# Sliding-window attention kept feature-major, three norms summed late, and every row scale from four narrow products: a two-layer decoder trunk on one core

## The chip, the cores and the metric

The kernel runs on one core of a Trainium2 chip. A core has a matrix engine (PE in the profile, its weight loads PEld), a vector engine (DVE), a scalar engine (ACT), a general engine (POOL) and an engine whose queue here only issues transfers (SP). The engines run side by side and wait for one another through semaphores; each works its own list of instructions in order. The metric is the device time of one launch in microseconds (us); a smaller number is better.

## The reference

Two macaron layers over 512 tokens of 1024 features, all in float32, and one norm at the end:

```
for i in 0, 1:
    h = h + 0.5 * swiglu(rms_norm(h, ln_ffn1[i]), ffn1_w_in[i], ffn1_w_out[i])      # 1024 -> 2 x 2816 -> 1024
    u = rms_norm(h, ln_mix[i])
    h = h + (mamba2(u) if i == 0 else sliding_window_attention(u))
    h = h + 0.5 * swiglu(rms_norm(h, ln_ffn2[i]), ffn2_w_in[i], ffn2_w_out[i])
out = rms_norm(h, final_norm)

rms_norm(x, w) = x * rsqrt(mean(x * x) + 1e-6) * w
swiglu(x, w_in, w_out) = (silu(gate) * up) @ w_out,  gate, up = split(x @ w_in)
attention: q, k, v = u @ w_qkv + b_qkv (16 query heads of 64, 4 key/value heads), rotary on q and k;
    logits = q k^T / 8 within the last 128 tokens; probs = softmax over the logits and one sink per head;
    out = (probs @ v) @ w_o + b_o
```

So there are seven row scales `rsqrt(mean(h*h) + eps)`: one ahead of each of the four feed-forward blocks, one ahead of each mixer and a last one.

## The kernel before

**Layout.** `h` lies feature-major: eight tiles `h0..h7` of 128 features by 512 tokens. The products are done to near float32 accuracy by splitting both sides into a rounded half and a rest (`hi`, `lo`) and doing three products of 512 columns (`mm3`, L328 to L330). `project` (L332) makes one 128 by 512 output from the eight `x` tiles: 24 products. The row scale is not applied to `x`; it multiplies the outputs when they leave PSUM, so a projection may run before its scale is known.

**Weights** stream from memory in the order of `weight_plan` into two raw buffers; ACT makes `whi` (L215), DVE `wlo` (L216), with four buffers each; the loads stand in SP's queue, beside `h` at the start.

**A norm's sum.** `make_x` (L258) is called when a tile `h[k]` is final: ACT scales it to `x` hi (L264), DVE makes `x` lo (L265), ACT squares it (L276) and POOL adds the square to `ss` (L277). The row scale from `ss` comes in two ways. `row_scale` (L312) splits `ss`, sums over the partitions with two products of 512 columns against a matrix of ones (L319, L320; the result stands in all partitions), and DVE takes the inverse root by three Newton steps on 128x512 tiles. `token_scale` (L291) does four products with one column (`psn`), so that the result is 128x4, DVE takes the root on that, and `spread` (L302) brings it to 128x512 with four products against the identity (`psb`) and a copy by ACT. Before, the first feed-forward block and the Mamba mixer take the second way, the other three blocks and the attention the first.

**Attention** (`swa`). Tokens of `SWA_ORDER` are walked: `K`, `V`, `Q` project, `v` turns V to token-major, `O` is a part of the output projection, and `a`, `b`, `c`, `d` are the steps of the generator `attend` for a pair of heads t. In `a`, PE makes the logits of both heads (`pss`, one head behind the other, L757), DVE adds the mask and finds the maximum (L761), ACT does the exponentials with their sum (L768). In `b`, PE turns the 2 x 7 blocks of probabilities (`pp`, L777) and ACT copies them out (`pT`). In `c`, PE multiplies the turned probabilities with the values, tokens on the partitions (`pav`, L787 and L789), and DVE multiplies with one over the sum (L792). In `d`, PE turns that back to feature-major (`pot`, L796), ACT and DVE split it to hi and lo. PSUM tiles come from two pools: `mm` with 4 buffers and `big` with 2; `pss`, `pp` and the tiles of the row scales are `big`.

**Order.** The program's text gives each engine its instructions; the framework then lists them anew per engine at compile time, by its own model of readiness. An engine never goes past an instruction that waits.

Of the kernel before, what the change touches and what calls it, by code (L numbers as in the profile page):

```python
# [18 lines left out]
S = 512  # L19
# [37 lines left out]


MAMBA_ORDER = mamba_order()
SWA_ORDER = """K0 V0 Q0 Q1 v0 a0 Q2 b0 a1 Q3 b1 c0 a2 K1 b2 c1 d0 a3 V1 b3 c2 d1 Q4 c3 d2 v1 O0:0 O0:1 Q5 d3 a4 Q6 b4 a5  # L60
O0:2 O0:3 Q7 b5 c4 a6 O1:0 O1:1 b6 c5 d4 a7 O1:2 O1:3 b7 c6 d5 O2:0 O2:1 c7 d6 O2:2 O2:3 d7 O3:0 O3:1 O3:2 O3:3
""".split()


def parse(tok):
    n, _, q = tok[1:].partition(":")
    return tok[0], int(n), int(q or 0)


def rows(k):  # L70
# [78 lines left out]
def trunk(ctx: ExitStack, tc: tile.TileContext, xT, pos, wflat, params, consts, out):  # L149
# [105 lines left out]
    x = [None] * KT  # L255
    norm = {}

    def make_x(k, n):  # L258
        w = pcol(P_LN + n * 8 + k)
        if k == 0:  # L260
            norm["ss"] = sm([128, S], name="ss", bufs=1)
# [9 lines left out]
        ss = norm["ss"]  # L271
        if k == 0:
            act.activation(ss, h[k], AF.Square)  # L273
        else:
            sq = t2([128, S], name="sq")
            act.activation(sq, h[k], AF.Square)  # L276
            pool.tensor_add(ss, ss, sq)  # L277

    def rsqrt(y, v, n, alloc):
        sh = alloc([128, n], I32, name=f"sh{n}")  # L280
# [28 lines left out]
        act.copy(rbc, pb)  # L309
        return rbc  # L310

    def row_scale():  # L312
        ss = norm["ss"]
        hi = t2([128, S], F32R, name="sshi")
        lo = t2([128, S], F32R, name="sslo")
        act.copy(hi, ss)
        dve.tensor_sub(lo, ss, hi.bitcast(F32))
        ps = big([128, S], name="psv")
        pe.matmul(ps, ones, hi, start=True, stop=False)  # L319
        pe.matmul(ps, ones, lo, start=False, stop=True)  # L320
        v = t2([128, S], name="nvw")
        dve.tensor_scalar(v, ps, EPS, None, op0=ALU.add)
        rbc = sm([128, S], name="rbc", bufs=1)
        rsqrt(rbc, v, S, t2)
        return rbc
# [6 lines left out]
    def project(eng=None):  # L332
# [4 lines left out]
            mm3(ps, hi[:, sl], lo[:, sl], (x[k][:, 0, :], x[k][:, 1, :]), k == 0, k == KT - 1)  # L337
        return ps

    def ffn(nxt, aside=None):  # L340
        gs = []
        for i in range(FT):
            if i == 8 and aside:
                aside()
            if i == 0 and nxt == 1:
                pg, pu = mm([128, S]), mm([128, S])
                for k in range(KT):
                    if k % 2 == 0:
                        hi, lo = next_w()
                    for j, ps in enumerate((pg, pu)):  # L350
                        sl = slice((2 * (k % 2) + j) * 128, (2 * (k % 2) + j + 1) * 128)
                        mm3(ps, hi[:, sl], lo[:, sl], (x[k][:, 0, :], x[k][:, 1, :]), k == 0, k == KT - 1)
                rbc = spread(token_scale(big, [norm["ss"]], 0, 4))
            else:
                pg = project()
                if i == 0:
                    rbc = row_scale()
                pu = project()
            t = t2([128, S], name="t")
            dve.tensor_mul(t, pg, rbc)  # L360
            act.activation(t, t, AF.Silu)
            dve.tensor_mul(t, pu, t)  # L362
            if i % 2 == 0:
                gs += halves("g")
            act.copy(gs[i][0], t)
            dve.tensor_sub(gs[i][1], t, gs[i][0].bitcast(F32))
# [347 lines left out]
        return cs, sn  # L714

    def swa(nxt, cs, sn):
        rbc = None
# [4 lines left out]
        def evac(b):  # L722
            nonlocal rbc
            ps = project()
            if rbc is None:
                rbc = row_scale()
            t = m4([128, S], name="qkv")
# [12 lines left out]
        def attend(t):  # L740
# [5 lines left out]
            rinv = sm([128, 4, 2], name="rinv")  # L746
            lgs = []
            for a in range(2):
                hs = slice(64 * a, 64 * a + 64)
                sink = pcol(P_SK + 2 * t + a)  # L750
                pss = big([128, 4, 256], name="pss")
                lg = m4([128, 4, 256], name="lg")
                lgs.append(lg)
                for i in range(4):
                    k0 = max(i - 1, 0) * 128
                    o = 128 if i == 0 else 0
                    pe.matmul(pss[:, i, o:], q[hs, i * 128:(i + 1) * 128], kT[kv][hs, k0:(i + 1) * 128],  # L757
                              start=True, stop=True)
                for i in range(4):
                    o = 128 if i == 0 else 0  # L760
                    dve.tensor_tensor_reduce(lg[:, i, o:], pss[:, i, o:], mask[:, o:], scale=0.125,  # L761
                                             scalar=-3.0e38, op0=ALU.add, op1=ALU.max,
                                             accum_out=mx[:, a, i:i + 1])
# [7 lines left out]
                dve.reciprocal(rinv[:, :, a], den[:, a, :])  # L771
            yield
            pTs = []
            for a in range(2):
# [7 lines left out]
            po = mm([128, 4, 2, 64], name="pav")  # L782
            for a in range(2):
                hs = slice(64 * a, 64 * a + 64)
                for i in range(4):
                    if i:
                        pe.matmul(po[:, i, a, :], pTs[a][:, 2 * i, :], vtok[kv][:, i - 1, hs],  # L787
                                  start=True, stop=False)
                    pe.matmul(po[:, i, a, :], pTs[a][:, 2 * i + 1, :], vtok[kv][:, i, hs],  # L789
                              start=i == 0, stop=True)  # L790
# [9 lines left out]
            act.copy(yt[0], pt)  # L800
            dve.tensor_sub(yt[1], pt, yt[0].bitcast(F32))
            yield

        chains = {}
        for tok in SWA_ORDER:
            s, n, part = parse(tok)
            if s == "Q":
                qT[n] = rope(evac(n))
            elif s == "K":
                kT[n] = rope(evac(8 + n))  # L810
            elif s == "V":
                vT = evac(10 + n)
            elif s == "v":
                pv = mm([128, 4, 128], name="pv")
                for c in range(4):
# [3 lines left out]
            elif s == "a":  # L819
                chains[n] = attend(n)  # L820
                next(chains[n])
            elif s in "bcd":
                next(chains[n])
            else:
                out_proj(part, n, pairs[n], n == 3, nxt, P_BO)
# [80 lines left out]
```

## Time and profile before

| | us |
|---|---|
| median of the runs (3; 2113.33 to 2117.11) | 2115.55 |
| the profiled execution, whole | 2119.48 |
| its span | 2117.7 |
| PE busy | 2083.3 (98%) |
| DVE busy | 1111.9 (53%) |
| ACT busy | 736.7 (35%) |
| POOL busy | 198.4 (9%) |

The profile's page comes first: busy times, the span in 40 slices, and the chain that ended last, of which PE is 91% and DVE 7%. With PE busy nearly throughout, what is left to look for is of three kinds: products that could go, stretches in which PE waits, and stretches in which its granted clock is at the lower level. Matmuls are pipelined: a row's own duration is longer than its distance to the next start, so distances between starts are used for the price of a product.

### The profile page before, as it was taken

Reading aid. Unit: us, or ns where it says so; the run is one execution under the profiler, and the core shown is the slowest. Engines: PE = TensorE matmul, PEld = TensorE weight load, DVE = VectorE, ACT = ScalarE, POOL = GpSimd, SP = SyncE. Lnnn points to the kernel's source line nnn. Section 1 sums busy time; section 2 is a strip of 40 time slices with the busy share of each in tenths; the row PEclk is TensorE's granted clock in tenths of the full one; section 3 lists DMA queues with packets and bytes.
Section 4 is the critical chain, followed back from the end, with each engine's and each line's share of the span. In section 5 each row is a group of like instructions: output and inputs, shape, how many; then the busy total and the mean of one; then the engine's idle time right before and its main releaser. Section 6 shows DMA issues by size and latency. Waiting matters only on the chain.

```text
span 2117.7 us, 24898 instructions
## 1 busy us (share of the span) xinstructions
PE 2083.3 (98%) x9967; PEld 1736.5 (82%) x9967; DVE 1111.9 (53%) x1709; ACT 736.7 (35%) x1088; POOL 198.4 (9%) x142
## 2 busy tenths in 40 slices
PE   8999999999999999999999999999999999999998
PEld 6888888888888887888888888888878878888887
DVE  6433433677888888443433535443365675334333
ACT  4332222454444444332222323322236443222222
POOL 2000001223222222000000000000110120000000
PEclk9999999999999999999999999999999999999999
DMA  5333232323333322333323333333321213333231
GB/s 163 95 100 100 88 100 84 115 90 107 100 97 98 92 83 80 93 97 99 97 92 93 97 100 100 94 97 92 96 93 41 60 51 99 100 100 92 92 98 67
DMA packets 58867, 197.62 MB, mean 93 GB/s; under 512 B 6656, under 2 KB 6912, under 8 KB 58752
## 3 DMA queue, kind: packets, MB, share of 16 engines
q1 hardware_dynamic: 58608, 196.03, 30.1%
q8 instruction: 78, 1.28, 0.2%
q14 instruction: 37, 0.30, 0.0%
q10 hardware_dynamic: 144, 0.00, 0.0%
HBM read 193.85 MB, written 2.16 MB: 93 GB/s over the span
## 4 chain that ended last, share of the span: by engine, by line
PE 91%; DVE 7%; ACT 1%; issue 1%; DMA 1%; POOL 0%; SPq 0%; ACTq 0%; DVEq 0%; POOLq 0%
PE mm L328 27%; PE mm L330 27%; PE mm L329 27%; PE psz L648 1%; PE psz L650 1%; PE psz L649 1%; PE psy L590 1%; DVE wlo L216 1%; DVE x L265 1%; PE pss L757 1%; DVE acc L518 1%; PE pav L789 1%; PE pp L777 1%; PE pav L787 0%; PE pso L593 0%
## 5 line engine op out<-in xcount | busy, mean ns | idle before, releaser
L215 ACT CAST whi<-wraw 128x1024 fp32r<-128x1024 f32 (+2 forms) x355 | 364.7, 1029 | 1084.2 <-PE mm L329 725.7
L328 PE MATMUL mm<-x,whi 128*128 128x512 f32 x1760 | 692.6, 394 | 5.8 <-DVE whi L213 5.7
L329 PE MATMUL mm<-x,whi 128*128 128x512 f32 x1760 | 690.0, 392 | 5.9 <-DVE x L265 5.9
L330 PE MATMUL mm<-x,wlo 128*128 128x512 f32 x1760 | 689.2, 392 | 1.1 <-DVE wlo L216 1.0
L216 DVE TENSOR_TENSOR wlo<-wraw,whi 128x1024 fp32r<-128x1024 f32 (+3 forms) x329 | 395.0, 1201 | 299.9 <-ACT whi L215 288.0
L329 PEld LDWEIGHTS mm<-x,whi 128*128 128x128 f32 x1760 | 332.7, 189 | 77.5 <-DVE x L265 9.1
L328 PEld LDWEIGHTS mm<-x,whi 128*128 128x128 f32 x1760 | 332.8, 189 | 76.3 <-ACT ss L273 5.7
L330 PEld LDWEIGHTS mm<-x,wlo 128*128 128x128 f32 x1760 | 332.6, 189 | 72.4 <-DVE wlo L216 2.0
L328 PE MATMUL mm<-ga,whi 128*128 128x512 f32 (+1 forms) x726 | 283.2, 390 | 0.0
L330 PE MATMUL mm<-ga,wlo 128*128 128x512 f32 (+1 forms) x726 | 280.7, 387 | 0.0
L329 PE MATMUL mm<-gb,whi 128*128 128x512 f32 (+1 forms) x726 | 279.4, 385 | 0.0
L277 POOL TENSOR_TENSOR ss<-ss,sq 128x512 f32<-128x512 f32 x48 | 72.5, 1510 | 1489.2 <-ACT sq L276 1487.9
L362 DVE TENSOR_TENSOR t<-mm,t 128x512 f32<-128x512 f32 x88 | 60.9, 692 | 270.2 <-PE mm L330 269.7
L360 DVE TENSOR_TENSOR t<-mm,rbc 128x512 f32<-128x512 f32 x88 | 60.6, 691 | 214.1 <-PE mm L330 213.1
L330 PEld LDWEIGHTS mm<-ga,wlo 128*128 128x128 f32 x726 | 136.2, 188 | 32.1
L329 PEld LDWEIGHTS mm<-gb,whi 128*128 128x128 f32 x726 | 136.2, 188 | 30.3
L328 PEld LDWEIGHTS mm<-ga,whi 128*128 128x128 f32 x726 | 136.1, 187 | 29.3
L216 POOL TENSOR_TENSOR wlo<-wraw,whi 128x1024 fp32r<-128x1024 f32 x30 | 73.4, 2448 | 218.1 <-ACT whi L215 218.1
L518 DVE SCALAR_TENSOR_TENSOR acc<-xp,par,acc 128x512 f32<-128x512 f32 x96 | 85.4, 889 | 1.4 <-ACT acc L516 1.3
L648 PE MATMUL psz<-whi,x 128*128 128x256 f32 x224 | 64.9, 290 | 5.3 <-DVE xp L514 5.3
L445 DVE TENSOR_TENSOR h<-mm,h 128x512 f32<-128x512 f32 x88 | 59.5, 685 | 14.0 <-PE mm L330 13.8
L650 PE MATMUL psz<-whi,x 128*128 128x256 f32 x224 | 64.1, 286 | 0.0
(211 smaller groups left out, 1902.1 us busy)
## 6 DMA issues: line engine op xcount, KB each, us to landing
wraw<-wflat SPq DMA_DIRECT2D x320, 512.0 KB, 3.6
wraw<-wflat SPq DMA_DIRECT2D x32, 384.0 KB, 3.0
abc<-actr SPq DMA_DIRECT2D x32, 256.0 KB, 5.0
h<-xT SPq DMA_DIRECT2D x8, 256.0 KB, 3.8
out<-out SPq DMA_DIRECT2D x4, 512.0 KB, 2.7
wraw<-wflat SPq DMA_DIRECT2D x4, 256.0 KB, 3.1
wraw<-wflat SPq DMA_DIRECT2D x2, 432.0 KB, 3.2
cst<-consts SPq DMA_DIRECT2D x1, 321.5 KB, 3.8
```

Of the source, the lines that this page charges most:

```text
L215: act.copy(hi[:, :w], r[:, :w])
L216: (eng or dve).tensor_sub(lo[:, :w], r[:, :w], hi[:, :w].bitcast(F32))
L277: pool.tensor_add(ss, ss, sq)
L328: pe.matmul(ps, whi, xt[0], start=first, stop=False)
L329: pe.matmul(ps, whi, xt[1], start=False, stop=False)
L330: pe.matmul(ps, wlo, xt[0], start=False, stop=last)
L360: dve.tensor_mul(t, pg, rbc)
L362: dve.tensor_mul(t, pu, t)
L445: dve.tensor_add(h[m], ps, h[m])
L518: dve.scalar_tensor_tensor(acc, xp[:, j:j + S], pcol(P_CW + t * 4 + j), acc, op0=ALU.mult, op1=ALU.add)
L648: pe.matmul(pz, x[k][:, 0, ts], hi[:, sl], start=k == 0, stop=False)
L650: pe.matmul(pz, x[k][:, 1, ts], hi[:, sl], start=False, stop=k == KT - 1)
```

## The change

Seven edits in one diff; the other functions are as before.

- The first block, the block after Mamba and the block after the attention have their squares kept in seven `side` buffers, and DVE adds them to `ss` (`add_late`); in the other norms POOL still adds.
- In every feed-forward block the row scale is `token_scale` after the first pair of projections and `spread` after the third. In the attention, three projections are held in PSUM: `token_scale` stands after `V0`, `spread` after `Q0`. `row_scale` is gone.
- The logits of both heads of a pair are made alternately, into two `pss` tiles that are there at the same time.
- The probabilities are multiplied with one over their sum before they are turned (L781, sixteen sets of four DVE instructions).
- The values are now the stationary side: `pav` is 64 features by 128 tokens for each head, the heads alternate, and the result is feature-major. The multiplication at the end and `pot` go.
- Projections of the attention leave PSUM into the `side` buffers.
- `SWA_ORDER` is written anew for three steps per pair.

```
@@ SWA_ORDER
-SWA_ORDER = """K0 V0 Q0 Q1 v0 a0 Q2 b0 a1 Q3 b1 c0 a2 K1 b2 c1 d0 a3 V1 ...
+SWA_ORDER = """K0 V0 r Q0 s Q1 v0 Q2 a0 Q3 a1 K1 b0 V1 a2 Q4 c0 b1 v1 Q5 a3 ...
@@ norms
+    def side(shape, dt=F32, name="s"):
+        return mpool.tile(shape, dt, name=name, tag="side", bufs=7)
+    def square(k, gather):
+        if k == 0:
+            norm["ss"] = sm([128, S], name="ss", bufs=1)
+            act.activation(norm["ss"], h[k], AF.Square)
+            norm["late"] = []
+            return
+        sq = (side if gather else t2)([128, S], name="sq")
+        act.activation(sq, h[k], AF.Square)
+        if gather:
+            norm["late"].append(sq)
+        else:
+            pool.tensor_add(norm["ss"], norm["ss"], sq)
+    def add_late():
+        for sq in norm.pop("late"):
+            dve.tensor_add(norm["ss"], norm["ss"], sq)
...
+        if n > 0:
+            square(k, n in (2, 5))
-    def row_scale():
...
@@ ffn
+            if i == 0:
+                first = first_pair() if nxt == 1 else (project(), project())
+                if norm["late"]:
+                    add_late()
+                rcol = token_scale(big, [norm["ss"]], 0, 4)
+                continue
+            pg = project()
+            if i == 1:
+                rbc = spread(rcol)
+                gate(0, *first, rbc, gs)
+            pu = project()
+            gate(i, pg, pu, rbc, gs)
@@ attend
+            pss = [big([128, 4, 256], name="pss") for _ in range(2)]
+            for i in range(4):
+                k0 = max(i - 1, 0) * 128
+                o = 128 if i == 0 else 0
+                for a in range(2):
+                    hs = slice(64 * a, 64 * a + 64)
+                    pe.matmul(pss[a][:, i, o:], q[hs, i * 128:(i + 1) * 128], kT[kv][hs, k0:(i + 1) * 128],
+                              start=True, stop=True)
...
+                for i in range(4):
+                    o = 128 if i == 0 else 0
+                    dve.tensor_scalar(lgs[a][:, i, o:], lgs[a][:, i, o:], rinv[:, a, i:i + 1], None, op0=ALU.mult)
...
-            o = t2([128, 4, 2, 64], name="o")
-            dve.tensor_mul(o, po, rinv.unsqueeze(3).to_broadcast([128, 4, 2, 64]))
-            yield
-            pt = mm([128, S], name="pot")
+            po = mm([128, S], name="pav")
             for i in range(4):
-                pe.transpose(pt[:, i * 128:(i + 1) * 128], o[:, i].rearrange("p a d -> p (a d)"), ident)
+                ts = slice(i * 128, (i + 1) * 128)
+                for b in ((2 * i, 2 * i + 1) if i else (1,)):
+                    for a in range(2):
+                        hs = slice(64 * a, 64 * a + 64)
+                        pe.matmul(po[hs, ts], vtok[kv][:, b // 2 + b % 2 - 1, hs], pTs[a][:, b, :],
+                                  start=b == max(2 * i, 1), stop=b == 2 * i + 1)
```

SP's queue at the start: `h` tiles, weight loads (`wraw`), constants and parameters. Before:

```order
L236 DMA h5_83<-xT 128x512
L236 DMA h6_84<-xT 128x512
L199 DMA wraw_102<-wflat 128x512
L236 DMA h7_85<-xT 128x512
L239 DMA cst_86<-consts 128x643
```

After:

```order
L236 DMA h5_83<-xT 128x512
L236 DMA h6_84<-xT 128x512
L236 DMA h7_85<-xT 128x512
L239 DMA cst_86<-consts 128x643
L240 DMA par_87<-params 128x356
L199 DMA wraw_102<-wflat 128x512
```

The last tile of `h` no longer stands behind the fourth weight load, which has to wait for a raw buffer.

DVE between Mamba's output projection and the next feed-forward block (`h7`, `x6`, `x7`: the last tiles of the residual and their lo halves; `wlo`: weight rests). Before:

```order
L216 TENSOR_TENSOR wlo_6528<-wraw_6408,whi_6527 128x1024
L265 SCALAR_TENSOR_TENSOR x6_6507<-h6_84,par_87,x6_6507 128x512
L265 SCALAR_TENSOR_TENSOR x7_6521<-h7_85,par_87,x7_6521 128x512
L216 TENSOR_TENSOR wlo_6584<-wraw_6414,whi_6583 128x1024
L317 TENSOR_TENSOR sslo_6559<-ss_6424,sshi_6558 128x512
L322 TENSOR_SCALAR nvw_6565<-psv_6562 128x512
```

After:

```order
L276 TENSOR_TENSOR ss_6427<-ss_6427,sq_6440 128x512
L454 TENSOR_TENSOR h7_85<-mm_6507,h7_85 128x512
L283 SCALAR_TENSOR_TENSOR x6_6502<-h6_84,par_87,x6_6502 128x512
L216 TENSOR_TENSOR wlo_6521<-wraw_6408,whi_6520 128x1024
L283 SCALAR_TENSOR_TENSOR x7_6515<-h7_85,par_87,x7_6515 128x512
L216 TENSOR_TENSOR wlo_6552<-wraw_6414,whi_6551 128x1024
L276 TENSOR_TENSOR ss_6427<-ss_6427,sq_6453 128x512
```

One of the seven adds now stands ahead of `x6` and `x7`, the other six behind `x7`, four of them ahead of another `wlo` and two behind it. On PE `psv` is gone from behind the first projection; `psn` stands behind the second and `psb` behind the third.

PE in the attention: the logits of one pair of heads, and its product with the values. Before (`pss_12205` and `pss_12223` are the two heads; the `pav` rows are the last of a pair):

```order
L757 MATMUL pss_12205<-qkv_11616,qkv_12023 128x128
L757 MATMUL pss_12205<-qkv_11616,qkv_12023 128x256 x3
L757 MATMUL pss_12223<-qkv_11616,qkv_12023 128x128
L757 MATMUL pss_12223<-qkv_11616,qkv_12023 128x256 x3
...
L787 MATMUL pav_12305<-vtok_11859,pT_12181 128x64
L789 MATMUL pav_12305<-vtok_11859,pT_12181 128x64
L796 MATMUL pot_12322<-cst_86,o_12198 128x128 x4
```

After (`pss_12231` and `pss_12232`, `pT_11565` and `pT_11575` are the two heads):

```order
L759 MATMUL pss_12231<-qkv_11549,qkv_11864 128x128
L759 MATMUL pss_12232<-qkv_11549,qkv_11864 128x128
L759 MATMUL pss_12231<-qkv_11549,qkv_11864 128x256
L759 MATMUL pss_12232<-qkv_11549,qkv_11864 128x256
...
L798 MATMUL pav_11699<-pT_11565,vtok_11340 64x128
L798 MATMUL pav_11699<-pT_11575,vtok_11340 64x128
```

The heads alternate in both groups of products, and nothing is turned back behind `pav`.

## Rows read from the trace of the kernel before

**Rows 1.** The page: busy time, share of the span and instructions of each engine.

```profile
PE 2083.3 (98%) x9967; PEld 1736.5 (82%) x9967; DVE 1111.9 (53%) x1709; ACT 736.7 (35%) x1088; POOL 198.4 (9%) x142
```

**Rows 2.** Stretches: length, busy (count) PE, PEld, DVE, ACT, POOL; clock; DMA; GB/s.

```profile
824.31:841.60 17.29, 14.97 (x51) 11.09 (x50) 15.08 (x18) 5.81 (x8) 6.27 (x4) 0.80 0.32 92
841.60:1198.23 356.63, 356.63 (x1561) 292.64 (x1561) 142.08 (x162) 103.19 (x128) 10.51 (x7) 1.00 0.32 96
1561.20:1736.05 174.85, 172.42 (x964) 144.06 (x964) 122.47 (x311) 85.73 (x212) 19.73 (x14) 0.98 0.18 55
1736.05:1753.35 17.30, 14.65 (x51) 10.95 (x50) 15.03 (x18) 6.22 (x10) 6.07 (x4) 0.80 0.28 80
```

**Rows 3.** Instructions in time, first 36 us: start, duration, engine, line, operation [idle before].

```profile
6.89 9.26 POOL L277 TENSOR_TENSOR ss<-ss,sq 128x512 f32<-128x512 f32 x6 [5.92 <-ACT sq L276]
8.43 1.77 DVE L265 SCALAR_TENSOR_TENSOR x<-h,par,x 128x512 fp32r<-128x512 f32 x1
12.29 0.43 SPq L236 DMA_DIRECT2D h<-xT  x1
15.58 0.72 ACT L264 ACTIVATE x<-h,par 128x512 fp32r<-128x512 f32 x1 [2.79 <-DMA h<-xT]
19.25 0.74 DVE L265 SCALAR_TENSOR_TENSOR x<-h,par,x 128x512 fp32r<-128x512 f32 x1
23.06 0.95 PE L295 MATMUL psn<-cst,ss 128*128 128x1 f32 x8
28.81 1.16 PE L306 MATMUL psb<-cst,rcol 128*128 128x128 f32 x8 [1.46 <-DVE rcol L289]
```

**Rows 4.** Instructions in time, from Mamba to the next block.

```profile
818.40 12.41 POOL L277 TENSOR_TENSOR ss<-ss,sq 128x512 f32<-128x512 f32 x7 [28.03 <-ACT sq L276]
822.83 1.18 DVE L265 SCALAR_TENSOR_TENSOR x<-h,par,x 128x512 fp32r<-128x512 f32 x1
827.89 3.47 DVE L265 SCALAR_TENSOR_TENSOR x<-h,par,x 128x512 fp32r<-128x512 f32 x2
829.72 0.50 PE L329 MATMUL mm<-x,whi 128*128 128x512 f32 x1 [0.91 <-DVE x L265]
831.42 0.50 PE L329 MATMUL mm<-x,whi 128*128 128x512 f32 x1 [0.73 <-DVE x L265]
```

**Rows 5.** PE in time, row scale between two feed-forward blocks.

```profile
1198.23 0.40 PE L319 MATMUL psv<-sshi,ones 128*128 128x512 f32 x1
1199.16 0.39 PE L328 MATMUL mm<-x,whi 128*128 128x512 f32 x1
```

**Rows 6.** Stretches of one pair's logits, `pss` alone: PE, PEld, DVE; clock; DMA.

```profile
1619.62:1620.38 0.76, 0.76 (x4) 0.70 (x5) 0.00 (x0) 1.00 0.00 0
1620.38:1621.15 0.77, 0.77 (x10) 0.74 (x9) 0.00 (x0) 1.00 0.00 0
1621.15:1622.10 0.95, 0.95 (x7) 0.56 (x3) 0.00 (x0) 1.00 0.00 0
```

**Rows 7.** PE in time, one pair's products with the values and what follows.

```profile
1629.21 0.33 PE L789 MATMUL pav<-vtok,pT 128*128 128x64 f32 x2
1632.28 0.61 PE L796 MATMUL pot<-cst,o 128*128 128x128 f32 x4
1632.64 0.47 PE L328 MATMUL mm<-x,whi 128*128 128x512 f32 x1
```

**Rows 8.** Attention: PE's longest wait (total, times, longest), and the stretch around it.

```profile
PE pss L757 <- DVE qkv L737: 1.8, 1, 1.8
1580.00:1592.00 12.00, 10.62 (x38) 8.17 (x39) 7.81 (x27) 6.25 (x21) 1.78 (x1) 0.72 0.14 44
```

**Rows 9.** DVE by line and shape, 1562 to 1726 us: busy, mean ns | idle before.

```profile
L761 DVE CUSTOM_DVE_ANT_0 lg<-pss,cst 128x256 f32<-128x256 f32 x48 | 17.8, 419 | 0.0
L792 DVE TENSOR_TENSOR o<-pav,rinv 128x512 f32<-128x512 f32 x8 | 5.5, 691 | 11.7 <-PE pav L789 11.7
```

**Rows 10.** DVE in time: four scalings of a 128x256 tile, in Mamba.

```profile
810.43 1.13 DVE L606 TENSOR_SCALAR y<-y,rn 128x256 f32<-128x256 f32 x4
```

More of the change, by code (lines that the diff above doesn't have):

```diff
@@ L66, in parse @@
     n, _, q = tok[1:].partition(":")
-    return tok[0], int(n), int(q or 0)
+    return tok[0], int(n or 0), int(q or 0)
 def rows(k):
@@ L270, in make_x @@
         x[k] = xt
[L271 to L277, printed above, removed]
+        if n > 0:
+            square(k, n in (2, 5))
     def rsqrt(y, v, n, alloc):
@@ L310, in spread @@
         return rbc
-    def row_scale():
[L313 to L325, printed above, removed]
     def mm3(ps, whi, wlo, xt, first, last):
@@ L338, in project, with gate, first_pair @@
         return ps
+    def gate(i, pg, pu, rbc, gs):
+        t = t2([128, S], name="t")
+        dve.tensor_mul(t, pg, rbc)
+        act.activation(t, t, AF.Silu)
+        dve.tensor_mul(t, pu, t)
+        if i % 2 == 0:
+            gs += halves("g")
+        act.copy(gs[i][0], t)
+        dve.tensor_sub(gs[i][1], t, gs[i][0].bitcast(F32))
+    def first_pair():
+        pg, pu = mm([128, S]), mm([128, S])
+        for k in range(KT):
+            if k % 2 == 0:
+                hi, lo = next_w()
+            for j, ps in enumerate((pg, pu)):
+                sl = slice((2 * (k % 2) + j) * 128, (2 * (k % 2) + j + 1) * 128)
+                mm3(ps, hi[:, sl], lo[:, sl], (x[k][:, 0, :], x[k][:, 1, :]), k == 0, k == KT - 1)
+            square(k, True)
+        return pg, pu
     def ffn(nxt, aside=None):
-        gs = []
+        gs, first = [], None
         for i in range(FT):
@@ L344, in ffn @@
                 aside()
[L345 to L366, printed above, removed]
+            if i == 0:
[10 more added lines that the diff above has]
+            gate(i, pg, pu, rbc, gs)
         for m in range(KT):
@@ L716, in swa @@
     def swa(nxt, cs, sn):
-        rbc = None
+        rbc, held = None, []
         swap = list(range(8, 16)) + list(range(8)) + list(range(16, 32))
@@ L720, in swa, with evac @@
         qT = {}
[L722 to L727, printed above, removed]
+        def evac(b, ps):
+            t = side([128, S], name="qkv")
             dve.tensor_mul(t, ps, rbc)
@@ L745, in attend @@
             den = sm([128, 2, 4], name="den")
-            rinv = sm([128, 4, 2], name="rinv")
+            rinv = sm([128, 2, 4], name="rinv")
             lgs = []
+            pss = [big([128, 4, 256], name="pss") for _ in range(2)]
[6 more added lines that the diff above has]
+                              start=True, stop=True)
             for a in range(2):
-                hs = slice(64 * a, 64 * a + 64)
                 sink = pcol(P_SK + 2 * t + a)
-                pss = big([128, 4, 256], name="pss")
                 lg = m4([128, 4, 256], name="lg")
@@ L754, in attend @@
                 for i in range(4):
-                    k0 = max(i - 1, 0) * 128
                     o = 128 if i == 0 else 0
[L757 to L761, printed above, removed]
+                    dve.tensor_tensor_reduce(lg[:, i, o:], pss[a][:, i, o:], mask[:, o:], scale=0.125,
                                              scalar=-3.0e38, op0=ALU.add, op1=ALU.max,
@@ L781, in attend @@
             yield
[L782 to L790, printed above, removed]
-            o = t2([128, 4, 2, 64], name="o")
-            dve.tensor_mul(o, po, rinv.unsqueeze(3).to_broadcast([128, 4, 2, 64]))
-            yield
-            pt = mm([128, S], name="pot")
-            for i in range(4):
-                pe.transpose(pt[:, i * 128:(i + 1) * 128], o[:, i].rearrange("p a d -> p (a d)"), ident)
+            po = mm([128, S], name="pav")
+            for i in range(4):
+                ts = slice(i * 128, (i + 1) * 128)
+                for b in ((2 * i, 2 * i + 1) if i else (1,)):
+                    for a in range(2):
+                        hs = slice(64 * a, 64 * a + 64)
+                        pe.matmul(po[hs, ts], vtok[kv][:, b // 2 + b % 2 - 1, hs], pTs[a][:, b, :],
+                                  start=b == max(2 * i, 1), stop=b == 2 * i + 1)
             if t % 2 == 0:
@@ L799, in attend @@
             yt = pairs[t // 2][t % 2]
-            act.copy(yt[0], pt)
-            dve.tensor_sub(yt[1], pt, yt[0].bitcast(F32))
+            act.copy(yt[0], po)
+            dve.tensor_sub(yt[1], po, yt[0].bitcast(F32))
             yield
@@ L806, in swa @@
             s, n, part = parse(tok)
-            if s == "Q":
-                qT[n] = rope(evac(n))
+            if s == "r":
+                rcol = token_scale(big, [norm["ss"]], 0, 4)
+            elif s == "s":
+                rbc = spread(rcol)
+                kT[0], vT = rope(evac(8, held[0])), evac(10, held[1])
+                qT[0] = rope(evac(0, held[2]))
+            elif s in "KVQ" and rbc is None:
+                held.append(project())
+            elif s == "Q":
+                qT[n] = rope(evac(n, project()))
             elif s == "K":
-                kT[n] = rope(evac(8 + n))
+                kT[n] = rope(evac(8 + n, project()))
             elif s == "V":
-                vT = evac(10 + n)
+                vT = evac(10 + n, project())
             elif s == "v":
@@ L821, in swa @@
                 next(chains[n])
-            elif s in "bcd":
+            elif s in "bc":
                 next(chains[n])
```

8 lines of the change are left out of this document (3 added, 5 removed).

## The prediction

> **What bounds the kernel now.** I read the page's first part, the busy times by stage, and then the instructions in time around each stretch in which PE waits. PE is busy for 98% of the span [rows 1], so time can come only from products that go or run side by side, from PE's waits, and from stretches at the lower clock. In a plain feed-forward stretch 1561 products take 356.63 us, 0.2285 each, at full clock [rows 2]; that is my price for a product of 512 columns. Measured with it, three places are slack.
>
> The two borders behind the mixers: from the first product of the next block, 48 products (two projections) are worth 48 x 0.2285 = 10.97 us and take 17.3 us with their row scale, at a mean clock of 0.80 of 2.4 GHz [rows 2]; the levels are 2.4 and 1.2, so a part of the stretch runs at 1.2. At the first border PE waits twice for DVE's `x` lo [rows 4], and the reader should see why: DVE's instruction takes 1.18 and 1.74 us (3.47 for two) while POOL is in its 12.4 us of adds, against 0.74 with POOL idle [rows 3, 4]. The start shows the same: 1.77 beside POOL, 0.74 without [rows 3]. The third place is the attention: 174.85 us at a mean clock of 0.98, with one wait of 1.8 us [rows 2, 8]; in the 12 us around that wait the clock is 0.72, so 12 x 0.28 = 3.4 us are lost to the level.
>
> **Part by part.** All sums are against the profiled execution: span 2117.7 us, whole 2119.48; the median of the runs is 3.9 below the whole.
>
> *Start.* POOL's adds go (9.26 us for six [rows 3]) and DVE takes seven more instructions. Up to the last weight rest of the first pair DVE then has, after the first `x` (from 6.3): seven `x`, three `whi`, three `wlo` and, by the order, four adds. At no more than 0.74 each that is 17 x 0.74 = 12.6, so at the latest 18.9; with narrow casts cheaper, nearer 17. `h7` no longer queues behind the fourth weight load: it was issued at 12.29 and ACT waited 2.79 us for it [rows 3]; now its transfer follows `h6`'s. The fourth load itself still waits for a raw buffer, as before. PE has some 12 to 20 products left then, so the pair ends at 20 to 21 where `psn` starts at 23.06 now: 2 to 3 us. The 1.46 us wait of `psb` [rows 3] goes too, since `psb` now stands at the end of the next projection. The other three adds end before `psn`; were they late, PE would wait at most 3 x 0.69. I take -4.0, bounds -2.0 and -4.6.
>
> *The two borders.* The adds go to DVE, but only one stands ahead of `x6` and `x7` at the first border and none at the second. With POOL idle, DVE needs about 0.69 + 0.74 for each `h` and its `x`, 1.43 us, and PE makes an output projection tile in 6 x 0.2285 = 1.37, so DVE ends some 2 us behind the last tile; PE has 18 products (4.1 us) to do before it needs `x6`. The waits go, and with them the fall of the clock. What is late next is `ss`: six adds (4.1 us) and two or three `wlo` (1.2 each) after `x7` make about 7 us, and PE has the rest of this projection and the whole next one (5.5) to cover it; the cushion is below 1 us, and a miss costs only its length. `psn` and `psb` are 0.95 + 1.16 = 2.1 us [rows 3]. So each border becomes 10.97 + 2.1 = 13.1 and gains 4.2: -8.4. Bounds: -2 (only POOL's slowing gone, the low level stays) and -9.4.
>
> *Feed-forward to feed-forward.* POOL still adds. The wide pair cost 0.93 with its wait [rows 5], the narrow sets 2.1: +1.2. DVE's twelve wide Newton instructions go, off PE's path. Bounds 0 and +1.2.
>
> *Attention, row scale.* +1.2 again for PE. DVE is spared about 7 us at the beginning, but the first evacuation waits for `psb` after `Q0`, some 13 us in.
>
> *Logits.* One pair's sixteen instructions take 2.48 us. Alone, the first head starts four in 0.76 us; in the next 0.77 us ten are in flight or start [rows 6]: the second head, on the other 64 rows, runs beside the first. Alternating from the beginning, both heads are done in the time of one, eight at 0.2, about 1.65: -0.8 a pair, -6.4 for eight. Bounds 0 and -6.9.
>
> *Products with the values.* 28 instructions take 3.07 us now, 0.11 each [rows 7]. Afterwards there are again 28, each head on its own 64 columns of the array. No row shows two column halves at once; the nearest is the pair of row halves above. In series: 3.07, no gain (a 128-column product is as long as the 128-column weight load that it swaps with). Side by side: 1.6 plus about 0.2 for changing over at both ends, -1.25 a pair, -10. I take -10; bounds 0 and -12.
> The Trainium skill, "TensorE: Matmul & The Clock Gate", in "Part 3: Packing small matmuls", says that a weight load overlaps a running product only when the row groups differ. Here both heads use all rows. But in the plain stretch weight loads of 292.64 us lie inside 356.63 us of products on the same rows [rows 2], so the trace does not bear it out as it stands; if it ruled the column halves, the sum would be that of the first rival. "TensorEngine Tiling (Array Packing)", "Key Properties", says that a change of the tiling mode drains the engine, which no row here prices for columns; sixteen changes at 0.1 are in my figure.
>
> *`pot`.* 0.36 a pair [rows 7]: -2.9 for eight.
>
> *Waits of the attention.* Gone: the 1.8 us and the 3.4 us of the low level: -5.2. New: DVE. From the spread on it has three held evacuations and their rotations, the 2.5 us maxima of each pair (0.42 each [rows 9]) and the new scalings (0.28 each [rows 10], some 2.1 us a pair, 16.6 in all; the final multiplication, 5.5 [rows 9], goes). Walking the order with these, the maxima of the first pair end about 33 us in, so that the second pair's logits wait some 1.2 us for their PSUM tiles, and the first turning waits some 1.6 us for the second pair's maxima, which stand behind the first pair's scalings. In the part with output projections DVE needs about 9.8 us a pair and PE 10.5. I take +3.5 for new waits; bounds +1 and +12.
>
> Attention: 1.2 - 6.4 - 10 - 2.9 - 5.2 + 3.5 = -19.8. All: -4.0 - 8.4 + 1.2 - 19.8 = -31.0, span 2086.7, and against the median 2115.55 - 31.0 = 2084.5.
>
> **Rivals.**
>
> *The column halves run one after the other.* Then 10 of the gain is gone, and some 1.5 of the new waits with it, as PE is slower: -22.5, 2093. For it: no row shows such a pair. Against it: the row halves do it. Chance 0.22.
>
> *DVE becomes the bound of the attention.* It is busy 122.5 of 174.85 us [rows 2]; some 126 would be left in 155, and it begins late. If two of its waits reach the 1.8 us behind which the clock fell here, each costs 1.8 + 3.4, together 10.4: -20.6, 2095. For it: the two tight places above. Against it: my waits are each below 1.8. Chance 0.16.
>
> *Slower.* The new scaling stands between the exponentials and the turning in every pair, and the turning heads PE's queue. If PE waits at `pp` in all eight pairs as it does once now, and the clock falls each time, that is 8 x 5.2 = 41.6 against 31.0: 2126. It decides from 3.9 us a pair. The order puts 14 us of PE work between `a` and `b` of a pair in the later part, against some 8 of the chain, so it needs DVE to fall behind by 6. Chance 0.03.
>
> *The late adds don't free the borders.* If DVE's adds, instead of POOL, keep `x6` and `x7` late, both borders stay as they are: -22.6, 2093. The order speaks against it. Chance 0.04.
>
> **How the numbers follow.** Forecast 0.55, rivals 0.22, 0.16, 0.03, 0.04. The forecast's own terms span 2076 to 2091; the rivals but the slow one lie at 2093 to 2095, with a few microseconds around each. 2075 to 2099 leaves out less than 2 in 10. A measurement of this kernel tells 0.2%, 4.2 us, from no change. Every case but the slow one is beyond that: faster 0.95, same 0.02, slower 0.03.
>
> **What would show it.** In the profile after: `x` lo at 0.74 us in all three gathered norms; both borders at a clock of 1.0 and near 13 us; a pair's sixteen `pss` in 1.7 us and its 28 `pav` in 1.8 (in 3.1 the first rival holds); no `psv` and `pot`; PE's waits in the attention for DVE, below 2 us each, and its length near 155. The prediction is wrong if a new stretch at 1.2 GHz stands in the attention, if a border still shows 0.8, or if `pav` costs more than now.

## The result, and the profile after

The changed kernel takes 2088.51 us (median of four runs, 2087.68 to 2088.58), beside 2116.33 (2113.33 to 2118.14) for the kernel before on the same chip: a ratio of 0.9869, 95% interval 0.9852 to 0.9886. Forecast were 2084.5 and 2075 to 2099. The span of the profiled execution is 2086.8 us, against a worked-out 2086.7. That agreement is closer than the single terms deserve: several were off, in both directions.

The page's first part, after [rows 1]:

```profile
PE 2058.6 (99%) x9991; PEld 1716.4 (82%) x9991; DVE 1093.8 (52%) x1782; ACT 738.5 (35%) x1088; POOL 166.1 (8%) x121
```

Since both kernels have 8034 products of the projection kind (`mm`), in the same sequence but for some of the attention's own, the two traces can be laid side by side by the number of the product: the time of product n after, less that of product n before, is what has been gained up to there. The stages, from the starts of the same products in both:

| stage (products) | before | after | difference | forecast |
|---|---|---|---|---|
| start, up to the 73rd product | 32.12 | 26.55 | -5.6 | -4.0 |
| rest of the first block, Mamba | 795.4 | 796.8 | +1.4 | 0 |
| border behind Mamba | 19.58 | 14.91 | -4.7 | -4.2 |
| feed-forward to feed-forward | 362.97 | 363.89 | +0.9 | +1.2 |
| next block, row scale of the attention | 362.98 | 363.89 | +0.9 | +1.2 |
| attention | 165.61 | 146.42 | -19.2 | -21.0 |
| border behind the attention | 20.29 | 15.36 | -4.9 | -4.2 |
| last block and end | | | +0.2 | 0 |
| sum | | | -30.9 | -31.0 |

Stretches of after, in the columns of [rows 2]: first border, plain feed-forward, attention, second border. The border stretches here hold 72 products and the whole row scale, as the spread now stands behind the third projection.

```profile
820.20:838.27 18.07, 18.07 (x89) 15.18 (x88) 13.22 (x28) 6.45 (x9) 0.00 (x0) 1.00 0.37 117
838.29:1194.99 356.70, 356.70 (x1564) 292.76 (x1563) 139.09 (x157) 102.81 (x128) 10.71 (x7) 1.00 0.33 96
1566.05:1709.60 143.55, 138.51 (x883) 110.82 (x882) 122.10 (x353) 83.95 (x213) 15.85 (x10) 1.00 0.19 60
1709.60:1727.84 18.24, 18.24 (x90) 15.30 (x89) 13.72 (x29) 7.12 (x10) 0.00 (x0) 1.00 0.40 116
```

Both borders run without a PE wait and at a clock of 1.00, where [rows 2] had 0.80. The plain stretch is unchanged (356.70 us for 1564 products, 356.63 for 1561 before), so the price of a product is too.

DVE in time at the first border, with POOL idle [rows 4]:

```profile
822.12 1.22 DVE L216 TENSOR_TENSOR wlo<-wraw,whi 128x1024 fp32r<-128x1024 f32 x1
823.29 0.75 DVE L283 SCALAR_TENSOR_TENSOR x<-h,par,x 128x512 fp32r<-128x512 f32 x1
...
825.09 2.86 DVE L276 TENSOR_TENSOR ss<-ss,sq 128x512 f32<-128x512 f32 x4
...
829.35 1.41 DVE L276 TENSOR_TENSOR ss<-ss,sq 128x512 f32<-128x512 f32 x2
832.08 0.16 DVE L311 TENSOR_SCALAR nv<-psn 128x4 f32<-128x4 f32 x1 [1.31 <-PE psn L308]
```

The last lo half takes 0.75 us instead of 1.74, and the last add ends at 830.76; PE starts `psn` at 831.09, when its second projection is done. The cushion was 0.3 us.

PE in time in the attention [rows 6, 7]: one pair's logits and one pair's products with the values, each with its neighbours.

```profile
1603.53 1.79 PE L759 MATMUL pss<-qkv 64*128 64x128 f32 x16
1605.25 0.50 PE L326 MATMUL mm<-x,whi 128*128 128x512 f32 x1
...
1610.93 1.75 PE L798 MATMUL pav<-pT,vtok 128*64 128x128 f32 x28
1612.61 1.75 PE L787 MATMUL pp<-cst,lg 128*128 128x128 f32 x14
```

From its first start to the next group's, `pss` is 1.72 us (2.48 before) and `pav` 1.68 (3.07 before). Around `pss` two distances are longer than 0.23: 0.32 ahead of it and 0.34 behind the first product after it. Groups that use the whole array (`psb`, `pv`, `pp`) have 0.23 ahead of them, but 0.31 to 0.32 behind the first product after them. So going over to half the array costs 0.09; most of the 0.1 on the way back stands behind any group of short products, and is not shown to come from the tiling.

PE's waits in the attention of after [rows 8]: total, times, longest.

```profile
PE pss L759 <- DVE mx L767: 1.8, 2, 0.9
PE pp L787 <- DVE mx L767: 1.6, 1, 1.6
PE pav L798 <- DVE h L454: 1.5, 1, 1.5
```

These are idle times; by the distances of starts, against the undisturbed pairs, the three places cost 2.4, 1.7 and 1.7 us. The first two are the waits that the prediction found by walking the order (at the second pair's logits and at the first turning); the third, a PSUM tile that DVE's sums into `h` free too late, was not foreseen. None is followed by a fall of the clock.

### The profile page after: what moved, and what is told of

Same layout as the page of the kernel before. It is cut to its first block, busy times and chain, and to the rows that moved or that the text cites. A ratio compares the mean times of both kernels' runs of the same rounds, so it can differ in the third digit from the quotient of the medians.

```text
span 2086.8 us, 24949 instructions
## 1 busy us (share of the span) xinstructions
PE 2058.6 (99%) x9991; PEld 1716.4 (82%) x9991; DVE 1093.8 (52%) x1782; ACT 738.5 (35%) x1088; POOL 166.1 (8%) x121
## 4 chain that ended last, share of the span: by engine, by line
PE 91%; DVE 6%; ACT 1%; issue 1%; POOL 0%; DMA 0%; ACTq 0%; SPq 0%; DVEq 0%; POOLq 0%
PE mm L326 28%; PE mm L328 27%; PE mm L327 27%; PE psz L657 1%; PE psz L659 1%; PE psz L658 1%; PE psy L599 1%; DVE acc L527 1%; DVE wlo L216 1%; PE pav L798 0%; PE pp L787 0%; ACT lg L774 0%; POOL qkv L741 0%; PE pso L602 0%; DVE lg L767 0%
## 5 line engine op out<-in xcount | busy, mean ns | idle before, releaser
L272 POOL TENSOR_TENSOR ss<-ss,sq 128x512 f32<-128x512 f32 x27 | 39.6, 1466 | 1523.7 <-ACT sq L268 1523.7
```

Source lines behind the costliest of these rows:

```text
L272: pool.tensor_add(norm["ss"], norm["ss"], sq)
```

## The experiments

Each is the changed kernel with one edit, unless it says otherwise; durations of groups are from their first start to the next group's. Undone parts come first.

**The heads of `pav` in turn.** The loop over `a` moves outside the loop over `i`.

```
+            for a in range(2):
+                hs = slice(64 * a, 64 * a + 64)
                 for i in range(4):
...
-                    for a in range(2):
```

> The changed kernel with one edit: the 14 products with the values of one head come before the 14 of the other instead of alternating; shape, number and buffers stay. Theory (the gain of pav is the two column halves of the array running side by side): 28 products go from the 1.68 us that the trace after shows to about 3.1 us a pair, 8 x 1.4 = 11 us more, of which DVE's waits give back 1 to 2 (1.5 us of them stand right ahead of pav): 2097 to 2100 us against 2088.5. Rival (the gain is the shape: 64 columns of weights loaded instead of 128, or the feature-major result): a pair stays at 1.7 us and the kernel at 2088.5.

Measured: 2096.33 us (2095.85 to 2097.69), a little below the range expected. One pair's products, PE in time:

```profile
1612.39 2.89 PE L798 MATMUL pav<-pT,vtok 128*64 128x128 f32 x28
```

2.82 us up to the next start in every pair, 0.1 for each product; alternating it is 0.06. Of the 1.39 us gained in a pair, 1.14 come from the alternation and 0.25 from the shape. The attention is 7.7 us longer: 9.1 less 1.4, the rest, of waits given back. The forecast's mechanism holds, with a small part for the rival. The Trainium skill, "TensorEngine Tiling (Array Packing)", "Key Properties", says that different tiles can load and multiply in parallel; the 1.68 against 2.82 us agree for column halves in float32. With the rule of "TensorE: Matmul & The Clock Gate", "Part 3: Packing small matmuls", weighed ahead of the forecast, these products on the same rows would have stayed in series; the trace does not bear it out.

**The heads of `pss` in turn**, by the same kind of edit.

> The changed kernel with one edit: the eight logit products of one head before the eight of the other. Theory (row halves run side by side only when neighbours in the queue are of different heads): sixteen products go from 1.72 back to about 2.5 us a pair, 8 x 0.76 = 6 us more; the first head's maxima can begin 0.9 us earlier, which takes up to 1 us off the waits of the second pair's logits and of the first turning (3.1 and 1.7 us in the trace after): 2092.5 to 2095 us. Rival (what was gained is the second PSUM tile being there, not the alternation): 1.7 us a pair, 2088.5.

Measured: 2091.59 us (2090.35 to 2092.02), less than expected. PE in time, one pair; then PE's waits of the attention:

```profile
1603.64 2.55 PE L759 MATMUL pss<-qkv 64*128 64x128 f32 x16
```

```profile
PE pp L787 <- DVE mx L767: 1.2, 1, 1.2
PE mm L327 <- DVE ob L804: 0.8, 2, 0.4
```

A pair takes 2.48 us again, 0.76 more, so the row halves do need the alternation. But the attention grows by only 3.0 us of the 6.1: the wait at `pav` is gone, and of the second pair's logits the 1.0 us ahead of the group is down to 0.1 and the 1.4 within it to 0.6. While DVE is late, half of what PE saves here comes back as waits.

**POOL adds at the two borders**: `square(k, n in (2, 5))` becomes `square(k, False)`.

> The changed kernel with one edit: in the norms behind the two mixers POOL adds the squares again; the place of the row scale stays. Theory (POOL's adds slow DVE's lo halves of x, PE waits for them and the granted clock falls): the lo halves take 1.2 to 1.7 us beside POOL instead of 0.74, PE waits about 1 us two times at each border, a stretch at 1.2 GHz follows; each border goes from 13 back to 16 to 17 us, 2095 to 2097 us in all. Rival (the border was freed by the row scale moving behind the second and third projection, and not by the adds): the borders stay within 1 us of 13, 2088 to 2090 us.

Measured: 2094.95 us (2093.43 to 2096.49). DVE and POOL in time at the first border, then both borders' stretches (up to the 73rd product) and PE's waits for the lo halves, which all stand at the two borders:

```profile
815.28 1.06 DVE L283 SCALAR_TENSOR_TENSOR x<-h,par,x 128x512 fp32r<-128x512 f32 x1
...
823.62 3.46 DVE L283 SCALAR_TENSOR_TENSOR x<-h,par,x 128x512 fp32r<-128x512 f32 x2
```

```profile
814.13 12.40 POOL L272 TENSOR_TENSOR ss<-ss,sq 128x512 f32<-128x512 f32 x7 [28.04 <-ACT sq L268]
```

```profile
820.00:842.00 22.00, 20.37 (x90) 16.24 (x88) 12.49 (x22) 7.14 (x9) 6.30 (x4) 0.92 0.31 96
1713.10:1736.00 22.90, 20.56 (x91) 16.39 (x90) 13.25 (x23) 8.11 (x11) 7.01 (x4) 0.93 0.30 92
```

```profile
PE mm L327 <- DVE x L283: 4.0, 4, 1.6
```

The slow lo halves, PE's waits and the low clock are back; the borders are 3.8 and 4.5 us longer. The later row scale alone does not free them.

**POOL adds at the start**: in `first_pair`, `square(k, True)` becomes `square(k, False)`.

> The changed kernel with one edit: POOL adds the squares of the first norm. The order then puts the last tile of h behind the fourth weight load again, as in the kernel before. Theory (both together made the start 5.6 us shorter): the first product with the third projection's successor stands 3.5 to 4.5 us later, since only the 1.6 us wait ahead of the spread stays away: 2092 to 2093 us. Rival (the place of the spread is what counts): 2089 to 2090 us, with psn at 19.5 to 20.5 us instead of 19.37.

Measured: 2091.95 us (2091.78 to 2092.42), start 24.42 instead of 20.83 from the first product to the 73rd. DVE, POOL, SP's queue and PE in time:

```profile
6.33 9.71 POOL L272 TENSOR_TENSOR ss<-ss,sq 128x512 f32<-128x512 f32 x6 [5.36 <-ACT sq L268]
...
8.32 1.77 DVE L283 SCALAR_TENSOR_TENSOR x<-h,par,x 128x512 fp32r<-128x512 f32 x1
...
12.18 0.43 SPq L236 DMA_DIRECT2D h<-xT  x1
...
22.95 0.95 PE L308 MATMUL psn<-cst,ss 128*128 128x1 f32 x8
```

So in these executions 3.6 us of the start are the adds with the earlier `h7` (3.4 by the medians), and 2.0 the place of the spread, of which the old wait of 1.46 [rows 3] is the larger part. The split is rough: eight other traces with the start of the changed kernel take 20.84 to 22.41 us for the same instructions. The two halves of the 3.6 were not told apart: the order moves the transfer whenever the adds move.

**One part alone, on the kernel before:** late adds by DVE behind the mixers, row scale where it was.

```
+            late = n in (2, 5)
+            sq = (side if late else t2)([128, S], name="sq")
...
+                    for sq in norm.pop("late"):
+                        dve.tensor_add(norm["ss"], norm["ss"], sq)
                     rbc = row_scale()
```

> The kernel before with one part of the change alone: behind the two mixers the squares are kept and DVE adds them, in the text behind the first projection and ahead of the wide row scale, which stays where it is. Theory (POOL's adds made the lo halves of x late): the lo halves take 0.74 us, PE's waits for them go; but seven adds on DVE (4.8 us) now stand between the last x and psv, and psv has only the rest of the first projection as cover, so part of the gain is given back as a wait at psv: each border goes from 17.4 to 14 to 16 us, 3 to 7 us less than before in all, ratio to before 0.9967 to 0.9986. Rival (adds alone free the border whatever stands behind): 12.9 us a border, 9 us less, ratio 0.9957.

Measured: ratio 0.9987 (0.9978 to 0.9997), 2112.58 us. The ratio lies at the edge of the theory's range, but not for its reason. The borders shrink by 5.5 and 5.7 us, more than the rival's 4.5 each; but PE then waits in a new place. PE's waits from the first border on, and DVE in time ahead of the longest:

```profile
PE mm L336 <- DVE t L370: 3.6, 2, 3.0
PE pss L767 <- DVE qkv L747: 1.8, 1, 1.8
```

```profile
1752.69 0.69 DVE L297 SCALAR_TENSOR_TENSOR rbc<-rw,rbc 128x512 f32<-128x512 f32 x1
1753.30 1.22 DVE L216 TENSOR_TENSOR wlo<-wraw,whi 128x1024 fp32r<-128x1024 f32 x1
1754.43 1.28 DVE L370 TENSOR_TENSOR t<-mm,rbc 128x512 f32<-128x512 f32 x2
```

The adds push the twelve wide Newton instructions back, so the first projection leaves PSUM only at 1754.4, some 20 us after PE is done with it; PE has no tile for the fifth, waits 3.0 us and runs 6.8 us at half clock behind it. The last block is 6.1 us longer. The late adds and the narrow row scale need one another.

The same run shows what a wait and the clock have to do with each other: the end of the old wait for `qkv`, the stretch behind it, and the stretch around the new wait.

```profile
1576.96 2.55 PE L767 MATMUL pss<-qkv 64*128 64x128 f32 x16 [1.82 <-DVE qkv L747]
```

```profile
1578.00:1590.00 12.00, 12.00 (x68) 9.65 (x66) 8.10 (x31) 8.52 (x24) 3.02 (x2) 1.00 0.14 46
1751.00:1763.00 12.00, 8.98 (x28) 6.90 (x27) 7.32 (x11) 4.83 (x6) 0.00 (x0) 0.72 0.22 74
```

Behind the wait of 1.8 us, where the clock had a mean of 0.72 in [rows 8], it stays at 1.00 here. A wait of that length does not always bring the fall.

**What the new waits of the attention come from.** Three edits, each with its own theory. (An evacuation is the copy of a projection out of PSUM by DVE and ACT; held ones are those of the three projections that wait in PSUM for the spread.)

The written order, one projection later for the second pair, the turnings and what follows:

```
-K0 V0 r Q0 s Q1 v0 Q2 a0 Q3 a1 K1 b0 V1 a2 Q4 c0 b1 v1 Q5 a3 Q6 c1 b2 Q7 a4 O0:0 O0:1 c2 b3 ...
+K0 V0 r Q0 s Q1 v0 Q2 a0 Q3 K1 a1 V1 b0 Q4 a2 v1 Q5 c0 b1 Q6 a3 Q7 c1 b2 O0:0 a4 c2 O0:1 b3 ...
```

> The changed kernel with only the written order of the attention altered: the second and later logits and the turnings stand one projection later behind the first pair, and the product with the values of pair 2 stands ahead of the second part output projection. Theory (the 6.6 us of new waits in the attention are DVE's arrears from the held evacuations at its beginning, and end once PE has other work there): the second pair's logits go from 3.1 to 1.7 us, the first turning from 3.2 to 1.5, the wait of 1.7 us ahead of the third product with the values shrinks below 0.5: 3.5 to 5.5 us less, 2083 to 2085 us. Rival (DVE, busy 126.5 of 148 us, bounds the attention, and the waits only move): 2087.5 to 2089.

Measured: 2091.67 us (2091.26 to 2093.31), the attention 2.9 longer. That theory fell. PE's waits in the attention:

```profile
PE pp L787 <- DVE mx L767: 4.1, 1, 4.1
PE mm L326 <- ACT oa L803: 1.8, 1, 1.8
```

The wait at the logits went as expected, but K1 leaves PSUM and is rotated ahead of the second pair's maxima now, so the first turning waits longer, and the clock falls behind it (0.86 on average in the 12 us from 1598 on).

ACT scales the probabilities: `act.activation(..., AF.Copy, scale=rinv[:, a, i:i + 1])` in the place of `dve.tensor_scalar`.

> The changed kernel with one edit: ACT instead of DVE multiplies the probabilities with one over their sum, 64 instructions of about 0.4 to 0.5 us. DVE loses 19.6 us of its 126.5 in the attention, ACT goes from 88 to some 116 of 148. Theory (DVE's new scalings cause the new waits): the wait of the first turning (1.6 us) and of the third product with the values (1.5) go, that of the second pair's logits, which stands ahead of any scaling, stays: 3 us less, 2085 to 2086. Rival (the waits are the held evacuations', ahead of any scaling): no more than 1 us less, 2087.5 to 2088.5; if ACT comes late with its copies of the turned blocks, 2090 or more.

Measured: 2096.79 us (2096.36 to 2097.84), the attention 7.9 longer. PE's waits there:

```profile
PE pss L759 <- ACT pT L789: 3.3, 5, 1.2
PE pav L798 <- DVE h L454: 2.8, 1, 2.8
PE pss L759 <- DVE mx L767: 1.7, 2, 0.9
```

DVE is relieved (107.1 of 154.3 us busy). The wait at the first turning is gone, as expected, and that at the second pair's logits untouched, as it stands ahead of any scaling; but ACT's copies of the turned blocks are now late, and the wait at `pav` has grown. So the scalings have a share in one wait of three, and ACT has no room for them.

The rotation wholly on DVE: `pool.tensor_mul(t, t, cs)` becomes `dve.tensor_mul(t, t, cs)`.

> The changed kernel with one edit: DVE instead of POOL multiplies with the cosine in the rotation of q and k. Theory (at the beginning of the attention DVE stands idle behind POOL in three rotations for 0.5 to 1.2 us, and its multiplication with the sine is slowed from 0.69 to 0.99 by POOL beside it): the maxima of the first pair end 1 to 2 us earlier and the waits of the second pair's logits and of the first turning lose 1 to 3 us together: 2085.5 to 2087.5 us. Rival (DVE's busy time is what counts; ten instructions of 0.69 are added): the waits grow by 1 to 3 us, 2089.5 to 2091.5.

Measured: 2083.57 us (2082.75 to 2084.49), ratio to before 0.9849; the attention is 4.4 us shorter, better than the theory's range. To see why, first DVE and then POOL in time in the changed kernel:

```profile
1582.33 0.69 DVE L740 TENSOR_TENSOR sh<-sh,sn 128x512 f32<-128x512 f32 x1
...
1584.22 0.69 DVE L742 TENSOR_TENSOR qkv<-qkv,sh 128x512 f32<-128x512 f32 x1 [0.99 <-POOL qkv L741]
...
1593.38 1.70 DVE L740 TENSOR_TENSOR sh<-sh,sn 128x512 f32<-128x512 f32 x1
```

```profile
1582.38 1.81 POOL L741 TENSOR_TENSOR qkv<-qkv,cs 128x512 f32<-128x512 f32 x1 [3.19 <-DVE sh L739]
1593.23 1.30 POOL L741 TENSOR_TENSOR qkv<-qkv,cs 128x512 f32<-128x512 f32 x1 [9.04 <-DVE sh L739]
```

Whichever starts second takes longer: POOL 1.81 instead of 1.30 when DVE began 0.05 us earlier, DVE 1.70 instead of 0.69 when POOL began 0.15 us earlier. All ten overlaps in the rotations go this way: POOL second six times, 1.73 to 1.81, and DVE second four times, 1.51 to 1.82. The Trainium skill states it on "SBUF — State Buffer", "Who interferes with whom": a DVE instruction with two inputs in SBUF contends with a GpSimd (here POOL) instruction that reads SBUF, and "Issue order, not op shape, decides who blocks." The trace agrees, here and for `x` lo beside the adds, which reads `h` and `x` hi. In this case's traces it is not only instructions with two inputs: at the start of the kernel before, DVE's casts to `whi`, which have one, take 1.01 and 1.50 us beside POOL's adds and 0.41 to 0.42 without. Over the attention, the two lines of the rotation in the changed kernel (busy, mean ns | idle before) and the same with POOL out of it:

```profile
L740 DVE TENSOR_TENSOR sh<-sh,sn 128x512 f32<-128x512 f32 x10 | 9.9, 986 | 0.2
L742 DVE TENSOR_TENSOR qkv<-qkv,sh 128x512 f32<-128x512 f32 x10 | 8.0, 796 | 4.7 <-POOL qkv L741 4.6
```

```profile
L740 DVE TENSOR_TENSOR sh<-sh,sn 128x512 f32<-128x512 f32 x10 | 6.9, 687 | 0.2
L741 DVE TENSOR_TENSOR qkv<-qkv,cs 128x512 f32<-128x512 f32 x10 | 6.8, 683 | 0.0
L742 DVE TENSOR_TENSOR qkv<-qkv,sh 128x512 f32<-128x512 f32 x10 | 6.8, 681 | 0.0
```

DVE gains 6.8 us of work and loses 4.2 of slowing (9.9 + 8.0 against 6.9 + 6.8) and 4.6 of idling: POOL's share cost DVE more than it took off it. With that the wait ahead of the second pair's logits is gone and the group takes 2.24 us instead of 3.09 (1.72 undisturbed), the wait at the first turning is gone and that at `pav` down to 0.6, the scalings still on DVE. One thing goes beside the edit: the order made at compile time now puts three projection products between the two heads' first turnings, so a part of that wait may be filled rather than removed.

**The better version.** The rotation on DVE, with `c2` one part output projection earlier (`O0:0 c2 O0:1 b3` for `O0:0 O0:1 c2 b3`), beside the changed kernel on the same chip.

> The changed kernel itself, beside the next one on the same chip. All theories: 2087.5 to 2089 us, attention (from the first product behind the spread to the last tiles of O3) 146.4 us.

> The kernel with the whole rotation on DVE, and in the attention's written order the product with the values of pair 2 stands one part output projection earlier. Theory (this product waits 0.6 us for its PSUM tile, which DVE's sums into h free; one step earlier the tile is free, and the copies of the turned blocks are there): that wait goes, 0.3 to 0.8 us less than the 2083.57 of the rotation alone, and 4.5 to 6 less than the changed kernel on the same chip. Rival (the next instructions wait the same 0.6 us for DVE): 2083 to 2084.

Measured: the changed kernel 2088.27 us (2087.2 to 2089.44), attention 146.32; the other 2082.9 (2082.81 to 2083.82), ratio to before 0.9842 (0.9826 to 0.9859). In its attention the list of waits as shown above is empty for PE. Against the rotation alone the attention is 0.2 us shorter (141.75), so the last edit is worth no more than that, though the 0.6 us wait at `pav` is gone; the start and Mamba differ by more between the two runs.

## Why the prediction was right

**The start** (-4.0 forecast, -5.6 measured, outside its bound of -4.6). `psn` came at 19.37 us, not at 20 to 21: the lo halves at 0.74 and `h7` behind `h6` left PE with only two short waits. The rest came as worked out. The size belongs in part to this execution: the eight other traces with this start have `psn` at 19.4 to 20.9 us and take up to 1.6 us more, so the gain was 4.0 to 5.6.

**The borders** (-8.4, -9.6). Each now costs 48 products and 1.62 us of row scale, 12.6 us instead of 13.1: `psn` and `psb` were priced at their durations, 2.1, and are 0.81 each by the distance of starts. The mechanism is shown from both sides, by POOL's adds put back and by the late adds put into the kernel before. One step was too light: that the wide Newton instructions go "off PE's path" is true of the kernel before only; with late adds they come onto it, for 6.1 us.

**Feed-forward to feed-forward** (+1.2, twice +0.9): the same price too high.

**Attention** (-19.8 with its row scale, -18.3). By its terms: logits -6.4 forecast, -6.1 measured (8 x 0.76); `pav` -10, -11.1 (8 x 1.39), with 0.25 a pair from the shape, not forecast; `pot` -2.9, -3.5 by the distances of starts; new waits +3.5, about +6.6. That last term is the one mis-sized: the two waits stood where the prediction put them, at 2.4 and 1.7 us by the distances of starts instead of 1.2 and 1.6, but its count of DVE's work names no slowing by POOL in the rotations, the very slowing that the borders had shown, and prices the scalings at 16.6 us, 0.28 each, where they take 19.6, 0.35 each; and the third wait, at a `pav` for a PSUM tile (1.7), was not seen. The other 0.9 are small ones in the later pairs. The first rival (column halves in series) is refuted by the pair of runs with and without alternation. The second (DVE the bound) did not come, though its cause was there: DVE made four waits of 0.9 to 1.6 us, without a fall of the clock behind them. DVE's total was forecast at some 126 us and is 126.5 in the 148 us from 1566 on, and yet the total does not tell its lateness: with POOL out of its way and more work it was in time. (With 19.6 us less work for it the kernel was slower, but there ACT came late.)

**Unforeseen:** +1.4 in Mamba, whose instructions are as before. Its `psz` waits are the same in both traces, but behind the first of them the clock of after falls, and that of before did not; behind the second it falls in both (mean clock of a stretch around it, after and then before):

```profile
456.00:464.00 8.00, 4.94 (x31) 4.74 (x30) 8.00 (x14) 2.19 (x4) 2.45 (x3) 0.79 0.48 134
```

```profile
461.00:469.00 8.00, 4.91 (x41) 4.71 (x40) 8.00 (x14) 2.66 (x5) 2.89 (x3) 1.00 0.46 134
```

This belongs to the execution and not to the change. In the better version, with the same code there, the clock falls behind the first wait alone, and the stage takes 795.6 us; in the nine other traces of the changed kernel and its variants, this one among them, it takes 796.6 to 797.1, with twice as long at 1.2 GHz (6.8 us).

**The step from the span to the median** is the one that put the time 4 us off. The sum was made against an execution of 2119.48 us, and then taken from the median of 2115.55. But about 10 of its 31 us were stretches at 1.2 GHz of that one execution (3.4 lost in each of three, by the mean clocks in [rows 2, 8]), and the run with the late adds shows that one of them need not be there. Taken from the execution it was made for, the same sum gives 2119.48 - 31.0 = 2088.5, the time measured; by the medians the change was worth 27 to 28 us. No other execution of the kernel before has a trace, but 27 of them have their mean granted clock on record: 21 take 2113.0 to 2115.7 us at 0.995 to 0.998, and six take 2119.3 to 2121.3 us at 0.992 to 0.994. The one that was profiled, 2119.48 us at 0.994, is like the six. A difference of 0.003 in the mean clock is some 6 us of 2115 (an estimate from these figures), about what lies between the two groups.

**The stated span of the forecast's own terms**, 2076 to 2091, is at its lower end close to the sum of the bounds (-38.8); the upper end is not worked out, as the bounds of 0 for `pav` and of +12 for the waits, which are the rivals' cases, would lead far above it.

## What to carry to other kernels

Price short products by the distance of their starts, alternate small products of the two row halves or the two column halves in the queue, and test that the alternation is what pays by undoing it alone. Before giving POOL an elementwise operation in SBUF, look at what DVE does at that moment: if DVE's instruction has two SBUF inputs, the one that starts second is held up (here a cast with one input was slowed too), and moving the work back to a busy DVE can gain. Take a gain that includes stretches at the lower clock from the execution that shows them, not from the median.

## What the hardware showed unexpectedly

Two column halves of 64 in float32, alternating, take 0.06 us for a 128-column product against 0.10 in turn. DVE's two-input instruction on 128x512 takes 0.69 us alone and 1.70 when POOL's (1.30) starts 0.15 us ahead of it. A PE wait of 1.8 us at the same place was followed by 6.8 us at 1.2 GHz in one kernel and by none in another.
